# Hybrid RG-LRU, retention and gated feed-forward block: another order of ScalarE's work in the gelu branch, head 1's values by seven half-size products among the scores

## The chip, the core and the metric

The kernel runs on one core of one Trainium2 chip. The metric is device time in microseconds of one execution, from its launch to its end on the device. The kernel before was timed three times: 1058.52, 1058.54 and 1058.54 us, median 1058.54 us.

A core has a matrix engine (TensorE, PE in the profile, its weight loads PEld), a vector engine (VectorE, DVE), a scalar engine for activation functions (ScalarE, ACT), a general one (GpSimd, POOL), and queues from which DMAs are issued (here mostly SyncE's, SP). Data lies in SBUF; matmul results go to PSUM, eight banks of 512 float32 columns on 128 partitions.

## What is computed

One block of a hybrid language model on 512 tokens with 16 learned meta tokens in front (T = 528), model width 1024, in float32. Cut to what matters:

```python
xn = rms_norm(h, norm_mix_g)
u_rnn, u_gate, q, k, v, g_ret, ga, gb = jnp.split(xn @ w_in, IN_SPLITS, axis=-1)

xr = causal_dwconv(u_rnn, rnn_conv_w, rnn_conv_b)
hr = rg_lru(xr, rg_a_w, rg_a_b, rg_x_w, rg_x_b, lru_lambda)    # 10 blocks of 128 channels
o_a = hr * gelu(u_gate)

o = retention(rotary(q), rotary(k) * 256 ** -0.5, v)            # 4 heads, dk 256, dv 512
o_b = head_rms(o) * silu(g_ret)

mixed = sigmoid(ga) * (o_a @ w_branch_rnn) + sigmoid(gb) * (o_b @ w_branch_ret)
h = h + mixed @ w_out
gate, val = split(causal_dwconv(rms_norm(h, norm_ffn_g) @ w_up, ffn_conv_w, ffn_conv_b))
h = h + (gelu(gate) * val) @ w_down
out = rms_norm(h, norm_final_g)[:, 16:]
```

In rg_lru, r and i are sigmoids of two small products per block, log_a = -8 r softplus(-lambda), a = exp(log_a), and the state follows s_t = a s_(t-1) + sqrt(1 - a^2) i x_t.

## The kernel before

**Precision.** Each float32 operand is split into two float16 parts, high and low (`split`, lines 93 to 96: ScalarE copies the scaled value to float16, VectorE subtracts that from the scaled value). A product is the sum of three float16 products, high by high, high by low, low by high (`SPLIT`). Weights come by DMA into one of three raw buffers (`wraw`) and are split into tiles of a pool of ten (`wsp`).

**Weight units.** Every weight matrix is cut into units of about 1 MB in the order of use (`units`). A plain unit makes two tiles in two steps. A unit marked `fast` is used in a Strassen-like scheme: a product of 2 x 2 blocks by seven half-size products instead of eight, on sums of blocks. Its `fast_steps` (lines 243 to 281) are five: half a tile, a tile, the block sums on VectorE (lines 262 to 264, 2048 columns in all), and two more tiles of the sums, marked late. `tick` emits the next step if the tiles from the current unit to that one number at most `ahead`; `get` emits all steps that are still missing of a unit.

**Order by hand.** From the first products to line 754 a hand-written order holds (`manual_schedule`): TensorE, ScalarE and VectorE each issue these instructions in the order of the program text. Behind that a planner orders the instructions, and may also pull later ones forward, between those written by hand too.

**The recurrent branch, lines 685 to 706.** Ten blocks n: `conv_product` (48 matmuls) into one of four PSUM accumulators of two banks (`acc`, from n = 2 on), `conv_taps` (one ScalarE and three VectorE operations on those sums), `conv_split`, and with a lag of three blocks `rnn_gates` (two products of six matmuls each into two accumulators, two sigmoids on ScalarE, a multiplication). Then softplus(-lambda) is made from a series of small operations (lines 709 to 727), which gives `cneg` and `cpos`.

**The gelu branch, lines 730 to 743.** Ten rounds n: `project` (48 matmuls) into an accumulator, one `tick`, Gelu from PSUM into SBUF on ScalarE, in rounds 0 to 2 the gates of blocks 7 to 9, and by a table (`SPREAD`) for five blocks at once: `rnn_tanh` and `rnn_decay` (ScalarE Tanh, Exp, two VectorE operations), `rnn_root` (ScalarE Sqrt), and in round 7 `rnn_scan` for blocks 0 to 4 (VectorE: a product and a scan over 528 tokens). ScalarE loads a function table when the next function isn't in the one it holds.

**Rotary, lines 761 to 792.** Eight units (q and k of four heads), each two projections of 48 matmuls, six VectorE operations on them, two splits. `between(i)` puts a scan of blocks 5 to 9 behind units 0 to 4, and `branch_a` (the product with the gelu result, and its split).

**Scores and values, lines 804 to 955 and 1148 to 1159.** `scores(h)`: three groups of products of rotated k and q into accumulators; VectorE multiplies by the decay, then they are split. `values(h)` for heads 0 and 1: 96 matmuls of 512 columns and 16 for the last 16 tokens. `fast_values(h)` for heads 2 and 3 (lines 960 to 1017): seven products of 24 matmuls of 256 columns on sums of the tokens' blocks, which `make_forms(0)` and `make_forms(1)` (lines 847 to 866) make once for all: for each, four additions, four more sums, four splits. The order of the calls is:

```python
    scores(0)
    values(0)
    make_forms(0)
    scores(1)
    scores(2)
    make_forms(1)
    values(1)
    scores(3)
    psum_layout(acc=2, bank=4)
```

Then come `retention_out`, the gated heads, the mixing, the output projection and the feed-forward part, which the change leaves alone.

Of the kernel before, what the change touches and what calls it, by code (L numbers as in the profile page):

```python
# [1 line left out]

# [51 lines left out]
def hybrid_block_kernel(ctx, tc, x, meta, norm_mix_g, w_in, conv_w, conv_b, rg_a_w, rg_a_b,  # L54
# [625 lines left out]
    def rnn_scan(n):  # L680
        r, t, xr = part(half_r, n), part(half_t, n), part(half_x, n)
        nc.vector.tensor_mul(t, t, xr)
        nc.vector.tensor_tensor_scan(xr, r, t, 0.0, op0=ALU.mult, op1=ALU.add)
# [25 lines left out]
    lv = vt1[:, 70:80]  # L709
    sp = const.tile([P, 8, NR], F32, name="sp")  # L710
    nc.vector.tensor_scalar(sp[:, 0], lv, -1.0, 0.0, op0=ALU.mult, op1=ALU.max)
    nc.scalar.activation(sp[:, 1], lv, AF.Abs)
    nc.scalar.activation(sp[:, 2], sp[:, 1], AF.Exp, scale=-1.0)
    nc.vector.tensor_scalar_add(sp[:, 3], sp[:, 2], 2.0)
    nc.vector.reciprocal(sp[:, 4], sp[:, 3])
    nc.vector.tensor_mul(sp[:, 4], sp[:, 4], sp[:, 2])
    nc.vector.tensor_mul(sp[:, 5], sp[:, 4], sp[:, 4])
    nc.vector.memset(sp[:, 6], 1.0 / 15.0)
    for m in (13, 11, 9, 7, 5, 3, 1):
        nc.vector.tensor_mul(sp[:, 6], sp[:, 6], sp[:, 5])  # L720
        nc.vector.tensor_scalar_add(sp[:, 6], sp[:, 6], 1.0 / m)
    nc.vector.tensor_mul(sp[:, 6], sp[:, 6], sp[:, 4])
    nc.vector.scalar_tensor_tensor(sp[:, 7], sp[:, 6], 2.0, sp[:, 0], op0=ALU.mult, op1=ALU.add)
    cneg = const.tile([P, NR], F32, name="cneg")
    cpos = const.tile([P, NR], F32, name="cpos")
    nc.vector.tensor_scalar_mul(cneg, sp[:, 7], -8.0)
# [4 lines left out]
    SPREAD = ((rnn_tanh, 2, 0), (rnn_decay, 3, 0), (rnn_tanh, 4, 5), (rnn_decay, 5, 5), (rnn_root, 7, 0), (rnn_scan, 7, 0), (rnn_root, 9, 5))
    for n in range(NR):
        ps = acc("ps")
        u, col = u_ug[n // 2], (n % 2) * P
# [2 lines left out]
        nc.scalar.activation(part(gate_g, n)[:, :TQ], run_of(ps, HQ),
                             AF.Gelu_apprx_tanh, scale=1.0 / (SW * S_XN))
# [106 lines left out]
    x_form_t = {}

    def make_forms(g):

        if not x_form_t:
            for i in range(2):  # L850
                x_form_t[i] = xslot([P, 4, 4, TW], F16, f"xs{i}")
        ks = slice(2 * g, 2 * g + 2)
        t = {}
        for i in range(2):
            for j in range(2):
                v = t[i, j] = work.tile([P, 2 * TW], F32, name="xt", tag="w").rearrange("p (k c) -> p k c", k=2)
                k0, c0 = 4 * j + 2 * g, XF + TH * i
                nc.vector.tensor_tensor(v, xh[:, k0:k0 + 2, c0:c0 + TW], xl[:, k0:k0 + 2, c0:c0 + TW], op=ALU.add)
        a11, a12, a21, a22 = t[0, 0], t[0, 1], t[1, 0], t[1, 1]
        nc.vector.tensor_tensor(a22, a22, a21, op=ALU.subtract)  # L860
        nc.vector.tensor_tensor(a21, a11, a21, op=ALU.subtract)
        nc.vector.scalar_tensor_tensor(a11, a22, -1.0, a11, op0=ALU.mult, op1=ALU.subtract)
        nc.vector.scalar_tensor_tensor(a12, a11, -1.0, a12, op0=ALU.mult, op1=ALU.subtract)
        for i, v in enumerate((a12, a22, a11, a21)):
            xs = x_form_t[i // 2]
            split(xs[:, 2 * (i % 2), ks], xs[:, 2 * (i % 2) + 1, ks], v, 1.0)

# [91 lines left out]

    def fast_values(h):  # L960

# [4 lines left out]
        vt = vv[h] = {}  # L966
        pa, pe, pb, pt = bank("pa"), bank("pe"), bank("pb"), acc("pv")[:, 0]

        def product(ps, wf, xf_, first=False):
            for a in range(2):  # L970
                for tt in range(2):
                    for k in range(2):
                        for ax, aw in SPLIT:
                            nc.tensor.matmul(ps[:, TH * tt:TH * tt + TH], x_form(xf_, ax, 2 * a + k, tt * P, P),  # L974
                                             ws[a](wf, aw, k),
                                             start=first and (a, tt, k, ax, aw) == (0, 0, 0, 0, 0),
                                             stop=a == 1 and k == 1 and ax == 1, skip_group_check=True)
# [807 lines left out]
```

## Time and profile before

| | |
|---|---|
| median of three runs | 1058.54 us |
| the profiled execution, its own time | 1058.55 us |
| its span, first to last instruction | 1056.8 us |
| mean granted TensorE clock | 0.999 |
| TensorE busy, matmuls | 1038.8 us |
| VectorE busy | 872.0 us |
| ScalarE busy | 594.3 us |
| DMA moved | 111.52 MB, mean 106 GB/s |

The profile is one execution. Each row of a view in order of time gives the start in us from the span's beginning, the time in us, the engine, the line of the kernel, the operation, what it writes and reads, its shape, and how many instructions are merged into the row; in square brackets stands how long the engine was idle before, and whom the profile names as releaser. "issue" means that the profile shows nobody. A merged row's time is from the first start to the last end. Matmuls overlap in time, so that TensorE's pace is better read from the starts of its weight loads.

### The profile page before, as it was taken

How to read it: one execution, taken by the hardware profiler on the slowest of the kernel's cores; microseconds unless marked ns; L12 is line 12 of the kernel's file. 1: busy time of each engine (PE TensorE's matmuls, PEld its weight loads, DVE VectorE, ACT ScalarE, POOL GpSimd, SP SyncE). 2: the span in 40 equal slices, each digit the busy share in tenths (PEclk: the TensorE clock that was granted, in tenths of full speed). 3: DMA queues.
4: the chain of work that ended last, by engine and by line, in shares of the span. 5: the costliest groups of instructions: out<-in, count | busy, mean ns of one | idle time of the engine just before them, and what ended most of it. 6: DMA issues, size and time to landing. Idle time of an engine off the chain costs nothing.

```text
span 1056.8 us, 21446 instructions
## 1 busy us (share of the span) xinstructions
PE 1038.8 (98%) x9187; PEld 866.2 (82%) x9187; DVE 872.0 (83%) x1327; ACT 594.3 (56%) x942; POOL 6.9 (1%) x20
## 2 busy tenths in 40 slices
PE   8999999999999999999999999999999999999997
PEld 6888888875588888888888886588888888888884
DVE  6885799989669999997797785479989898988965
ACT  7558973444356758666454453375555555454432
POOL 2000000000000000000000000000000000000000
PEclk9999999999999999999999999999999999999999
DMA  9241253331013132334333355032433324114312
GB/s 295 94 132 58 81 180 120 123 120 41 1 41 113 49 106 74 102 111 154 102 115 120 111 209 180 1 120 81 160 102 99 120 81 144 58 61 145 96 41 80
DMA packets 109311, 111.52 MB, mean 106 GB/s; under 512 B 5674, under 2 KB 101136, under 8 KB 109216
## 3 DMA queue, kind: packets, MB, share of 16 engines
q1 hardware_dynamic: 108640, 109.74, 32.5%
q8 instruction: 72, 1.18, 0.5%
q10 hardware_dynamic: 288, 0.27, 0.1%
q0 software_dynamic: 288, 0.14, 0.1%
q14 instruction: 23, 0.19, 0.1%
HBM read 108.04 MB, written 2.10 MB: 104 GB/s over the span
## 4 chain that ended last, share of the span: by engine, by line
PE 74%; DVE 15%; ACT 8%; issue 2%; DMA 0%; ACTq 0%; DVEq 0%
PE ps L434 27%; PE P L1603 10%; PE pa L886 9%; DVE wt L95 4%; PE pe L886 4%; PE ps L1320 4%; PE pm L434 3%; PE ps L448 3%; PE pb L886 2%; PE ps L950 2%; PE pa L1490 2%; ACT wt L94 2%; PE ps L1040 2%; PE pa L974 1%; DVE raw L262 1%
## 5 line engine op out<-in xcount | busy, mean ns | idle before, releaser
L434 PEld LDWEIGHTS <-wt 128*128 128x128 f16 x3840 | 372.8, 97 | 53.4 <-issue 1.3
L95 DVE SCALAR_TENSOR_TENSOR wt<-raw,wt 128x1024 f16<-128x1024 f32 (+2 forms) x286 | 310.4, 1102 | 54.0 <-ACT wt L94 52.9
L94 ACT ACTIVATE wt<-raw 128x1024 f16<-128x1024 f32 (+2 forms) x286 | 267.8, 958 | 117.8 <-PE P L1603 23.1
L886 PEld LDWEIGHTS <-wt 128*128 128x128 f16 x2016 | 195.3, 97 | 32.4 <-issue 5.7
L434 PE MATMUL ps<-x2h,wt 128*128 128x258 f16 (+1 forms) x1184 | 196.2, 273 | 0.0
L434 PE MATMUL ps<-xh,wt 128*128 128x258 f16 (+4 forms) x1056 | 177.5, 275 | 1.6 <-DVE t L773 1.6
L434 PE MATMUL ps<-x2l,wt 128*128 128x256 f16 (+1 forms) x592 | 161.0, 272 | 0.0
L434 PE MATMUL ps<-xl,wt 128*128 128x256 f16 (+4 forms) x528 | 140.8, 274 | 0.0
L1603 PE MATMUL P<-wt,act 128*128 128x256 f16 x792 | 88.3, 273 | 0.0
L1603 PEld LDWEIGHTS <-act 128*128 128x128 f16 x792 | 77.4, 98 | 9.0
L886 PE MATMUL pa<-xs,wt 128*128 128x258 f16 x576 | 71.3, 273 | 1.9 <-ACT kept L892 1.5
L1468 DVE SCALAR_TENSOR_TENSOR cv<-ps,vt,cv 128x512 f32<-128x512 f32 x80 | 59.5, 747 | 9.1 <-ACT cv L1466 8.5
L434 PE MATMUL pm<-oa,wt 128*128 128x256 f16 (+1 forms) x480 | 54.1, 273 | 0.0
L262 DVE TENSOR_TENSOR raw<-raw 128x1024 f32<-128x1024 f32 x43 | 52.5, 1220 | 0.7
L886 PE MATMUL pa<-ob,wt 128*128 128x257 f16 x384 | 45.7, 274 | 0.6 <-ACT last L892 0.5
L1320 PE MATMUL ps<-wt,mx 128*128 128x512 f16 x192 | 44.3, 379 | 0.0
L950 PE MATMUL ps<-wt,xh 128*128 128x512 f16 x128 | 38.3, 379 | 0.7 <-ACT qk L94 0.5
L1466 ACT ACTIVATE cv<-ps,vt,vt 128x512 f32<-128x512 f32 x40 | 30.5, 766 | 11.9 <-PE ps L434 11.9
L1490 PEld LDWEIGHTS <-wt 128*128 128x128 f16 x336 | 32.6, 97 | 4.4
L1320 PEld LDWEIGHTS <-mx 128*128 128x128 f16 x192 | 17.6, 98 | 18.5
L94 ACT ACTIVATE qk<-t 128x514 f16<-128x514 f32 (+1 forms) x16 | 10.2, 638 | 39.6 <-DVE t L775 39.6
L448 PEld LDWEIGHTS <-wt 128*128 128x128 f16 x288 | 27.9, 97 | 5.0 <-issue 0.5
(327 smaller groups left out, 1504.5 us busy)
## 6 DMA issues: line engine op xcount, KB each, us to landing
raw<-in_w_in SPq DMA_DIRECT2D x36, 1024.0 KB, 5.1
raw<-in_w_up SPq DMA_DIRECT2D x24, 1024.0 KB, 5.2
raw<-in_w_down SPq DMA_DIRECT2D x48, 256.0 KB, 3.7
raw<-in_w_branch_ret SPq DMA_DIRECT2D x16, 512.0 KB, 4.9
raw<-in_w_in SPq DMA_DIRECT2D x12, 512.0 KB, 4.8
raw<-in_w_branch_rnn SPq DMA_DIRECT2D x8, 640.0 KB, 4.7
raw<-in_w_out SPq DMA_DIRECT2D x4, 1024.0 KB, 5.1
xin<-in_x SPq DMA_DIRECT2D x4, 512.0 KB, 5.8
```

Of the source, the lines that this page charges most:

```text
L94: a = nc.scalar.activation(hi, src, AF.Copy, scale=s)
L95: b = nc.vector.scalar_tensor_tensor(lo, src, s, hi, op0=ALU.mult, op1=ALU.subtract)
L262: nc.vector.tensor_tensor(pair, pair, rv[:, :, right].rearrange("p (h k) c -> p h k c", h=2), op=ALU.add)
L434: nc.tensor.matmul(half_of(ps, halves, hf), w(aw, k, col, P), src(ax, k, c0, n), start=k == 0 and (aw, ax) == (0, 0), stop=k == nk - 1 and ...
L448: mm = nc.tensor.matmul(half_of(ps, halves, hf), w(aw, k, col, P), src(ax, k, c0, n), start=k == 0 and (aw, ax) == (0, 0), stop=k == KD - ...
L886: nc.tensor.matmul(ps[:, :n], ws[k // 4](wf, aw, k % 4), src(xf_, ax, k), start=first and k == 0 and (aw, ax) == (0, 0), stop=k == last_k ...
L950: nc.tensor.matmul(pb, xf(ax, k, XF + j0, nb), w(aw, k % 4, 0, 512), start=i == 0, stop=i == 23)
L1320: nc.tensor.matmul(ps[:, n], mx[k][:, a, c0:c0 + P], wo[k // 2](aw, k % 2, n * 512, 512), start=k == 0 and (a, aw) == (0, 0), stop=k == ks ...
L1466: nc.scalar.activation(vv_, taps[2], AF.Identity, scale=vt2[:, 96 + ch:97 + ch], bias=bias)
L1468: nc.vector.scalar_tensor_tensor(vv_, taps[j], vt2[:, 48 * j + ch:48 * j + ch + 1], vv_, op0=ALU.mult, op1=ALU.add)
L1490: nc.tensor.matmul(ps[:, :258], w(wf, aw, k), x2_form(xf_, ax, k), start=first and k == 0 and (aw, ax) == (0, 0), stop=k == 3 and aw == 1, ...
L1603: nc.tensor.matmul(pd[:, 256 * tt:256 * tt + 256], t[:, ax, c0 + tt * P:c0 + tt * P + P], w(wf, aw, i), start=q % 6 == 0 and tt == 0 and i ...
```

## The change

- Softplus: its Abs and Exp are issued in round 2 of the recurrent branch, its VectorE operations, 18 instead of 24, three at a time behind `conv_taps` of rounds 3 to 7.
- Tanh of blocks 0 to 5 is issued in rounds 8 and 9 of the recurrent branch, of blocks 6 to 9 in rounds 0 to 2 of the gelu branch.
- Gelu: in rounds 5, 8 and 9 from PSUM as before; in the others ScalarE copies the sums to SBUF (`AF.Copy`), and Gelu is done later in place, in rounds 5 and 8. In a round the work of the tables `FIRST` and `THEN` stands ahead of that copy.
- The gates of blocks 8 and 9 both stand in round 1.
- Eight of ten scans are in the gelu branch (rounds 7 to 9), two are left in `between`.
- `make_forms(0)` stands in round 0 of the gelu branch, behind its `tick`; `make_forms(1)` behind `values(0)`.
- Head 1's weight units are `fast`, and `fast_values(1)` takes the place of `values(1)`: behind each product it lets one group of `scores(2)`, then of `scores(3)`, be issued. For it the PSUM layout with two accumulators and four single banks begins before it and not behind `scores(3)`; the products for the last tokens get a bank of their own. `ahead` is 12 there.

```diff
     def add_v(h):
-        if h >= 2:
-            u_v[h] = [unit(4, 512, [(2 * j, 0, kmaj(w_in, 4 * j + 2 * a, 2, o_v + 512 * h, 512)) for j in range(2)],
-                           fast=True) for a in range(2)]
+        if h == 0:
+            u_v[h] = [unit(4, 512, [(0, 0, kmaj(w_in, 4 * a, 4, o_v, 512))]) for a in range(2)]
             return
-        u_v[h] = [unit(4, 512, [(0, 0, kmaj(w_in, 4 * a, 4, o_v + 512 * h, 512))]) for a in range(2)]
+        u_v[h] = [unit(4, 512, [(2 * j, 0, kmaj(w_in, 4 * j + 2 * a, 2, o_v + 512 * h, 512)) for j in range(2)],
+                       fast=True) for a in range(2)]
...
+    def softplus_exp():
+        lv = vt1[:, 70:80]
+        nc.vector.tensor_scalar(sp[:, 0], lv, -1.0, 0.0, op0=ALU.mult, op1=ALU.max)
+        nc.scalar.activation(sp[:, 1], lv, AF.Abs)
+        nc.scalar.activation(sp[:, 2], sp[:, 1], AF.Exp, scale=-1.0)
+
+    def softplus_rest():
+        nc.vector.tensor_scalar_add(sp[:, 3], sp[:, 2], 2.0)
+        nc.vector.reciprocal(sp[:, 4], sp[:, 3])
+        nc.vector.tensor_mul(sp[:, 4], sp[:, 4], sp[:, 2])
+        yield
...
         conv_taps(n, ps)
+        if LAG <= n < 8:
+            next(series)
+        if n >= 8:
+            for i in range(3 * (n - 8), 3 * (n - 8) + 3):
+                rnn_tanh(i)
...
         if n == 2:
+            softplus_exp()
             tick()
...
+    def make_forms(g):
...
+        nc.vector.scalar_tensor_tensor(a12, a11, -1.0, a12, op0=ALU.mult, op1=ALU.subtract)
+        for i, v in enumerate((a12, a22, a11, a21)):
+            xs = x_form_t[i // 2]
+            split(xs[:, 2 * (i % 2), ks], xs[:, 2 * (i % 2) + 1, ks], v, 1.0)
...
-    SPREAD = ((rnn_tanh, 2, 0), (rnn_decay, 3, 0), (rnn_tanh, 4, 5), (rnn_decay, 5, 5), (rnn_root, 7, 0), (rnn_scan, 7, 0), (rnn_root, 9, 5))
+    FIRST = {0: (rnn_tanh, (6,)), 1: (rnn_tanh, (7,)), 2: (rnn_tanh, (8, 9)), 5: ("gelu", range(5)), 6: (rnn_root, range(5)), 7: (rnn_root, range(5, 10)),
+             8: ("gelu", (6, 7))}
+    THEN = {2: (rnn_decay, (0, 1)), 3: (rnn_decay, range(2, 6)), 4: (rnn_decay, range(6, 10)),
+            7: (rnn_scan, range(3)), 8: (rnn_scan, (3, 4)), 9: (rnn_scan, range(5, 8))}
+
+    def gate_gelu(i, src=None, s=1.0):
+        g = part(gate_g, i)[:, :TQ]
+        nc.scalar.activation(g, g if src is None else src, AF.Gelu_apprx_tanh, scale=s)
+
     for n in range(NR):
         ps = acc("ps")
         u, col = u_ug[n // 2], (n % 2) * P
         project(ps, get(u), col, xf, HQ, KD)
         tick()
-        nc.scalar.activation(part(gate_g, n)[:, :TQ], run_of(ps, HQ),
-                             AF.Gelu_apprx_tanh, scale=1.0 / (SW * S_XN))
-        if n < LAG:
-            rnn_gates(NR - LAG + n)
-        for f, n0, m0 in SPREAD:
-            if n == n0:
-                for i in range(m0, m0 + 5):
-                    f(i)
+        if n == 0:
+            make_forms(0)
+        for what in (FIRST, THEN):
+            f, ms = what.get(n, (None, ()))
+            for m in ms:
+                (gate_gelu if f == "gelu" else f)(m)
+        if n in (5, 8, 9):
+            gate_gelu(n, run_of(ps, HQ), 1.0 / (SW * S_XN))
+        else:
+            nc.scalar.activation(part(gate_g, n)[:, :TQ], run_of(ps, HQ), AF.Copy, scale=1.0 / (SW * S_XN))
+        for i in ((7,), (8, 9))[n] if n < 2 else ():
+            rnn_gates(i)
...
     def between(i):
-        if i < 5:
-            rnn_scan(5 + i)
+        if i < 2:
+            rnn_scan(8 + i)
...
-    scores(0)
+    rest(scores(0))
     values(0)
-    make_forms(0)
-    scores(1)
-    scores(2)
     make_forms(1)
-    values(1)
-    scores(3)
+    rest(scores(1))
     psum_layout(acc=2, bank=4)
+    ahead[0] = 12
+    fast_values(1, chain(scores(2), scores(3)))
     ahead[0] = 9
```

More of the change, by code (lines that the diff above doesn't have):

```diff
@@ L1 @@
 from contextlib import ExitStack, nullcontext
+from itertools import chain
 import concourse.bass as bass
@@ L683, in rnn_scan @@
         nc.vector.tensor_tensor_scan(xr, r, t, 0.0, op0=ALU.mult, op1=ALU.add)
+    cneg = const.tile([P, NR], F32, name="cneg")
+    cpos = const.tile([P, NR], F32, name="cpos")
+    sp = const.tile([P, 8, NR], F32, name="sp")
+    def softplus_exp():
[8 more added lines that the diff above has]
+        yield
+        nc.vector.tensor_mul(sp[:, 5], sp[:, 4], sp[:, 4])
+        nc.vector.tensor_scalar_mul(sp[:, 6], sp[:, 5], 1.0 / 15.0)
+        for m in (13, 11, 9, 7, 5, 3):
+            nc.vector.scalar_tensor_tensor(sp[:, 6], sp[:, 6], 1.0 / m, sp[:, 5], op0=ALU.add, op1=ALU.mult)
+            if m in (13, 7):
+                yield
+        nc.vector.scalar_tensor_tensor(sp[:, 6], sp[:, 6], 1.0, sp[:, 4], op0=ALU.add, op1=ALU.mult)
+        yield
+        nc.vector.scalar_tensor_tensor(sp[:, 7], sp[:, 6], 2.0, sp[:, 0], op0=ALU.mult, op1=ALU.add)
+        nc.vector.tensor_scalar_mul(cneg, sp[:, 7], -8.0)
+        nc.vector.tensor_scalar_mul(cpos, sp[:, 7], 8.0)
+        yield
+    series = softplus_rest()
     LAG = 3
@@ L706, in hybrid_block_kernel @@
             conv_split(n)
[L709 to L726, printed above, removed]
@@ L727, in hybrid_block_kernel @@
-    nc.vector.tensor_scalar_mul(cpos, sp[:, 7], 8.0)
-    ahead[0] = 6
-    SPREAD = ((rnn_tanh, 2, 0), (rnn_decay, 3, 0), (rnn_tanh, 4, 5), (rnn_decay, 5, 5), (rnn_root, 7, 0), (rnn_scan, 7, 0), (rnn_root, 9, 5))
+    x_form_t = {}
+    def make_forms(g):
+        if not x_form_t:
+            for i in range(2):
+                x_form_t[i] = xslot([P, 4, 4, TW], F16, f"xs{i}")
+        ks = slice(2 * g, 2 * g + 2)
+        t = {}
+        for i in range(2):
+            for j in range(2):
+                v = t[i, j] = work.tile([P, 2 * TW], F32, name="xt", tag="w").rearrange("p (k c) -> p k c", k=2)
+                k0, c0 = 4 * j + 2 * g, XF + TH * i
+                nc.vector.tensor_tensor(v, xh[:, k0:k0 + 2, c0:c0 + TW], xl[:, k0:k0 + 2, c0:c0 + TW], op=ALU.add)
+        a11, a12, a21, a22 = t[0, 0], t[0, 1], t[1, 0], t[1, 1]
+        nc.vector.tensor_tensor(a22, a22, a21, op=ALU.subtract)
+        nc.vector.tensor_tensor(a21, a11, a21, op=ALU.subtract)
+        nc.vector.scalar_tensor_tensor(a11, a22, -1.0, a11, op0=ALU.mult, op1=ALU.subtract)
+        nc.vector.scalar_tensor_tensor(a12, a11, -1.0, a12, op0=ALU.mult, op1=ALU.subtract)
+        for i, v in enumerate((a12, a22, a11, a21)):
+            xs = x_form_t[i // 2]
+            split(xs[:, 2 * (i % 2), ks], xs[:, 2 * (i % 2) + 1, ks], v, 1.0)
@@ L802, in hybrid_block_kernel, with rest @@
     SCP = [(0, SOFF[0]), (1, SOFF[1]), (2, SOFF[2]), (2, SOFF[2]), (2, SOFF[2])]
+    def rest(run):
+        for _ in run:
+            pass
     def scores(h):
@@ L832, in group @@
                 split(sb[:, 0, o:o + n], sb[:, 1, o:o + n], f[:, :n], 1.0)
-        group([(0, 0, 0, 257), (1, 0, 257, 257)])
-        group([(0, 1, 0, T - I0[1]), (1, 2, 0, T - I0[2])])
-        group([(0, 3, 0, T - I0[3]), (1, 4, 0, T - I0[4])])
+        yield group([(0, 0, 0, 257), (1, 0, 257, 257)])
+        yield group([(0, 1, 0, T - I0[1]), (1, 2, 0, T - I0[2])])
+        yield group([(0, 3, 0, T - I0[3]), (1, 4, 0, T - I0[4])])
     xlast = const.tile([P, KD, 2, NM], F16, name="xlast")
@@ L843, in hybrid_block_kernel @@
     vv, oraw, rstd, ob, ob_a11 = {}, {}, {}, [], []
[L845 to L866, printed above, removed]
     def x_form(nm, a, k, c0, n):
@@ L958, in hybrid_block_kernel, with fast_values @@
     nc.vector.tensor_scalar_mul(xneg, xlast[:, 0:4], -1.0)
-    def fast_values(h):
+    def fast_values(h, others=()):
         ws = [get(u) for u in u_v[h]]
@@ L966, in fast_values @@
         vt = vv[h] = {}
-        pa, pe, pb, pt = bank("pa"), bank("pe"), bank("pb"), acc("pv")[:, 0]
+        others = iter(others)
+        pa, pe, pb = bank("pa"), bank("pe"), bank("pb")
+        pt = bank("pv") if h == 1 else acc("pv")[:, 0]
         def product(ps, wf, xf_, first=False):
@@ L978, in product @@
             tick()
+            next(others, None)
         def keep(ps):
@@ L1034, in retention_out @@
                     o = SOFF[b] + s0 - I0[b] - SCP[b][1]
-                    if h < 2 or b == 4:
+                    if h == 0 or b == 4:
                         vd = vt[b][:, va, d * P:(d + 1) * P]
@@ L1212, in mix_first @@
         mix_a.append(m)
-    def rest(run):
-        for _ in run:
-            pass
     def gate_a(i, run=None):
```

## The prediction

> **What bounds the kernel now.** I read the page's busy shares and its chain first, then the weight loads in order of time, then ScalarE and VectorE beside them.
>
> ```profile
> span 1056.8 us, 21446 instructions
> ...
> PE 1038.8 (98%) x9187; PEld 866.2 (82%) x9187; DVE 872.0 (83%) x1327; ACT 594.3 (56%) x942; POOL 6.9 (1%) x20
> ...
> PE 74%; DVE 15%; ACT 8%; issue 2%; DMA 0%; ACTq 0%; DVEq 0%
> ```
>
> TensorE sets the end. A change pays only by taking matmul time away or by closing a gap between matmuls; ScalarE, at 56%, pays only where TensorE waits for it. Every f16 matmul here has its own weight load, so the loads (PEld) in order of time show each gap:
>
> ```profile
> 80.86 5.28 PEld L434 LDWEIGHTS <-wt 128*128 128x128 f16 x48
> 86.15 1.33 PEld L434 LDWEIGHTS <-gw 128*128 128x128 f16 x12
> 87.50 5.28 PEld L434 LDWEIGHTS <-wt 128*128 128x128 f16 x48
> 92.79 1.33 PEld L434 LDWEIGHTS <-gw 128*128 128x128 f16 x12
> ...
> 100.77 68.99 PEld L434 LDWEIGHTS <-wt 128*128 128x128 f16 x624
> 170.64 10.74 PEld L434 LDWEIGHTS <-wt 128*128 128x128 f16 x96 [0.88 <-DVE t L773]
> 182.64 42.74 PEld L434 LDWEIGHTS <-wt 128*128 128x128 f16 x384 [1.26 <-issue]
> ```
>
> The gelu branch (ten rounds, the first at 80.86) has no gap, though ScalarE is full there: TensorE runs on over 624 loads from 100.77. So **relieving ScalarE is worth nothing by itself**. The gaps, 0.88 and 1.26 us, come in the rotary stage, the first put down to VectorE.
>
> **The change part by part.** *The sums in the gelu branch.* Up to the end of that branch each engine keeps the program's order. Rows of ScalarE, then of VectorE:
>
> ```profile
> 85.61 0.20 ACT L712 ACTIVATE sp<-vt 128x10 f32<-128x10 f32 x1
> ...
> 87.23 1.04 ACT L94 ACTIVATE wt<-raw 128x1024 f16<-128x1024 f32 x1
> ...
> 89.58 0.60 ACT L737 ACTIVATE rnn<-ps 128x514 f32<-128x514 f32 x1
> 90.20 1.28 ACT L663 ACT_TABLE_LOAD   x1
> 91.50 0.70 ACT L663 ACTIVATE rnn<-ps,vt 128x528 f32<-128x528 f32 x1
> 92.09 0.69 ACT L663 ACTIVATE gi<-ps,vt 128x528 f32<-128x528 f32 x1
> ...
> 103.60 3.23 ACT L668 ACTIVATE rnn<-rnn,cpos 128x528 f32<-128x528 f32 x5
> ...
> 128.46 0.60 ACT L737 ACTIVATE rnn<-ps 128x514 f32<-128x514 f32 x1
> ...
> 244.28 1.75 ACT L94 ACTIVATE xs<-xt 128x544 f16<-128x544 f32 x3
> ```
>
> ```profile
> 91.69 1.22 DVE L95 SCALAR_TENSOR_TENSOR wt<-raw,wt 128x1024 f16<-128x1024 f32 x1
> 92.82 0.70 DVE L665 TENSOR_TENSOR rnn<-rnn,gi 128x528 f32<-128x528 f32 x1
> ...
> 113.14 0.70 DVE L674 TENSOR_TENSOR a<-rnn 128x528 f32<-128x528 f32 x1
> 113.87 0.71 DVE L675 SCALAR_TENSOR_TENSOR rnn<-a,rnn 128x528 f32<-128x528 f32 x1
> ...
> 236.27 0.72 DVE L858 TENSOR_TENSOR xt<-xh,xl 128x544 f32<-128x544 f16 x1
> ...
> 238.16 1.99 DVE L858 TENSOR_TENSOR xt<-xh,xl 128x544 f32<-128x544 f16 x3
> ...
> 243.53 0.72 DVE L863 SCALAR_TENSOR_TENSOR xt<-xt 128x544 f32<-128x544 f32 x1
> ```
>
> The order shows at 91.69: the low half of a weight split whose high half ended at 88.27 waits until the small softplus operations are through. In the new round 0 ScalarE gets the weight split, then the four splits of make_forms(0), tanh(6), and only then the copy that empties round 0's sums from PSUM. The first of the four splits needs a12, the last of eight VectorE operations. Worked out:
>
> - The weight split takes the place of L712 at 85.61 and ends at 86.65. Its low half starts at 86.69 and holds VectorE 1.13 (91.69 to 92.82), to 87.82.
> - Eight operations follow at 0.635 each (three end to end in 1.99, the last taking 0.72), one of them 0.10 later because it reads the result just made (113.14 to 113.87 against 0.63). a12 is there at 87.82 + 7 x 0.635 + 0.10 + 0.72 = 93.1. Until then ScalarE stands still.
> - Four splits at 0.55 each (1.75 for three) run to 95.3, tanh(6) at 0.63 (3.23 for five) to 96.0, the copy at 0.60 to 96.6.
>
> TensorE meets this at 92.79. PSUM has four accumulators, and then all are held: round 0's sums, the two gates of block 7, round 1's sums. The gates of block 8 come next and wait for the copy, from 92.79 to 96.6: **3.8 us**. Behind the copy ScalarE has the sigmoids of block 7 (96.45, 97.04), round 1's weight split (97.63), tanh(7) and round 1's copy, which ends at 99.8. The fourth of the gate products of blocks 8 and 9 (0.67 each, half of 1.33) waits for that one: it could start at 96.6 + 3 x 0.67 = 98.6, so 1.25 more. Round 2 starts at 100.5 instead of 92.79 + 4 x 0.67 = 95.5: **+5.0 us**. Bounds of this unseen wait: 0 if the copy does not queue behind the splits; 7.7 if the eight operations take what they took at 236.27 to 244.25 among others (8.0 instead of 5.3). I take 5.0, since the hand-written order puts nothing between them. Later rounds carry no gates; a copy there may lie three rounds behind.
>
> *Tanh, softplus, in-place gelu, table loads.* Most table loads (1.28 each) go and seven 0.60 operations come; ScalarE bounds nothing in that branch apart from the wait above: 0. The 18 small series operations run three to a block in a hole like this one, at 0.21 a step:
>
> ```profile
> 79.78 0.71 DVE L95 SCALAR_TENSOR_TENSOR xs<-rnn,xs 128x528 f16<-128x528 f32 x1 [0.71 <-ACT xs L94]
> 88.44 0.17 DVE L721 TENSOR_SCALAR sp<-sp 128x10 f32<-128x10 f32 x1
> 88.65 0.17 DVE L720 TENSOR_TENSOR sp<-sp 128x10 f32<-128x10 f32 x1
> 39.18 0.64 ACT L94 ACTIVATE xs<-rnn 128x528 f16<-128x528 f32 x1 [2.76 <-DVE rnn L647]
> ```
>
> 3 x 0.21 = 0.63 fits under 0.71; without that cover it would be some 3 us of VectorE, not of TensorE. Abs, exponential and table load, 1.7, fit into the 2.76 before 39.18.
>
> *Scans moved ahead.* Three of the five scans between rotary units go into the gelu branch:
>
> ```profile
> 137.80:182.64 44.84, 43.26 (x387) 37.17 (x385) 44.84 (x57) 20.31 (x26) 0.00 (x0) 1.00 0.45 149
> 182.64:225.40 42.76, 42.73 (x384) 37.19 (x385) 39.81 (x57) 18.45 (x26) 0.00 (x0) 1.00 0.43 139
> 133.55 1.26 DVE L683 TENSOR_TENSOR_SCAN rnn<-rnn 128x528 f32<-128x528 f32 x1
> ```
>
> In these window rows (length, then TensorE, loads, VectorE) VectorE is full up to 182.64, and free for 3 us after. A scan and its product cost about 1.9, three 5.7, well over the 2.14 of both gaps. Nothing else is late there: the next unit's accumulators come free with that same VectorE work. **-2.1 us.** Bounds 0 and -2.1, for the stage has no other gap to close.
>
> *Head 1's values.* Chain pieces of the plain form, then of the seven products of head 2, then windows of the stage and of heads 2 and 3:
>
> ```profile
> 260.05 15.38 PE ps L950 x71
> 275.43 0.98 PE ps L942 x16
> 335.60 0.86 PE pv L1008 x25
> 339.19 2.62 PE pe L974 x24
> 225.40:285.20 59.80, 58.87 (x369) 30.92 (x367) 50.16 (x101) 23.77 (x46) 0.00 (x0) 1.00 0.08 27
> 320.00:341.70 21.70, 20.65 (x212) 17.44 (x210) 19.78 (x25) 13.38 (x20) 0.00 (x0) 1.00 0.34 104
> 368.40:389.90 21.50, 20.56 (x211) 17.36 (x210) 19.73 (x26) 13.63 (x19) 0.00 (x0) 1.00 0.32 105
> ```
>
> Plain: 96 matmuls at 0.217 plus 0.98 for the last 16 tokens = 21.8. New: 7 x 2.62 = 18.3, plus 40 small ones (25 in 0.86) at 1.4 = 19.7. **-2.1 us**, if nothing waits. VectorE, at 1.13 per 1024 columns, gets per unit 1.5 more low halves and 2048 columns of sums (4.0; two units 8.0) and three additions of 512 (1.7), and loses twelve operations of make_forms (7.6): some 2.1 into 9.6 free (59.80 less 50.16). Scores stand between the products and give VectorE time. Bounds: -2.1, and 0, for heads 2 and 3 take 21.7 and 21.5 for this very work, no less than the plain form. I take -2.1, because there VectorE is free for only 2 us.
>
> **Sum:** the profiled execution took 1058.55 (span plus 1.75; the median is 1058.54). 1058.55 + 5.0 - 2.1 - 2.1 = **1059.4**. A measurement of this kernel can tell about 0.2%, 2.1 us, from no change, so I forecast no difference.
>
> **The rivals.**
>
> *The half-size products wait for their weights* as heads 2 and 3 do: then the third term is 0 and the time 1061.5, slower. It decides itself at the third product, whose form is cut last and whose buffers come free only when head 0's values are done; in between lie scores(1) (8076 columns at 0.217 per 512: 3.4), two products (5.2) and two score groups (7116 columns: 3.0), 11.6 us. For it: the two windows. Against it: 9.6 us free.
>
> *ScalarE's queue does not hold the copy back*, so the sums cost nothing: 1058.55 - 2.1 - 2.1 = 1054.4, faster. For it: round 6 ends on TensorE at 100.77 + 192 x 0.1106 = 122.0 (68.99 for 624 loads), its result leaves PSUM at 128.46, and no gap follows. Against: in rounds 0 and 1 gates take the accumulators that gave round 6 its time.
>
> *The wait slows the clock.* Quoted windows show a granted clock of 1.00, gaps up to 1.26 included; 3.8 us of idling is not in the trace. Were the 24 gate matmuls behind it (2.67) at half pace, the time would be 1062.1. The Trainium skill, "TensorE: Matmul & The Clock Gate", section "HAM oscillation — how this bites in real kernels", says that an idle gap over about 3.4 us halves the clock; no row of before bears on it.
>
> *VectorE stays late in the rotary stage*: the second term is 0, 1061.5. Against: 5.7 us less to do, and TensorE arrives 5.0 later.
>
> **How the numbers follow.** Forecast 0.50 (of it 0.03 faster, 0.39 same, 0.08 slower), products waiting 0.17 (0.06 same, 0.11 slower), no hold-back 0.22 (faster), clock 0.06 (slower), rotary 0.05 (0.02 same, 0.03 slower). Together faster 0.25, same 0.47, slower 0.28. The forecast's own range is 1057.0 to 1061.5: planner-placed work after the branch can shift a gap of 0.5 to 1.2 either way. The range given, 1054.0 to 1062.0, takes in most of the other cases, the middle of the no-hold-back case too.
>
> **What would show it.** Right: a gap of about 3.8 us before the gates of block 8 and 1.2 before the last gate of block 9, both released by ScalarE's copies; round 2 some 5 us late; no gap over 0.3 near 170 and 182 (shifted by 5); head 1's 168 products in 18.3 us of their own. Wrong: no gap before round 2, or gaps over 1 us among head 1's products.

## The result and the profile after

The changed kernel takes **1061.28 us** (median of 14 runs, 1060.23 to 1061.87) against 1058.58 us for the kernel before on the same chip: ratio 1.0023, 95% interval 1.0016 to 1.003. That is 2.7 us slower, just over what a measurement can tell from no change. The forecast was 1059.4 us.

The page of the changed kernel: its span, the busy shares, the granted clock over 40 slices, and the shares of the chain that ended last.

```profile
span 1059.5 us, 21649 instructions
...
PE 1039.5 (98%) x9283; PEld 875.2 (83%) x9283; DVE 881.8 (83%) x1332; ACT 591.1 (56%) x947; POOL 6.9 (1%) x20
...
PEclk9998999999999999999999999999999999999999
...
PE 83%; DVE 11%; ACT 4%; issue 2%; ACTq 0%; DVEq 0%
```

ScalarE lost 3 us of work and VectorE gained 10, yet the span grew by 2.7: the shares don't tell why. One digit does: the fourth slice of PEclk, around 80 to 106 us, fell to 8. So the weight loads are read in order of time again (start, duration, engine, line, operation, operands, count, idle time before it):

```profile
85.93 1.33 PEld L435 LDWEIGHTS <-gw 128*128 128x128 f16 x12
87.27 5.28 PEld L435 LDWEIGHTS <-wt 128*128 128x128 f16 x48
92.56 0.10 PEld L435 LDWEIGHTS <-gw 128*128 128x128 f16 x1
96.75 4.94 PEld L435 LDWEIGHTS <-gw 128*128 128x128 f16 x23 [4.09 <-issue]
101.77 128.01 PEld L435 LDWEIGHTS <-wt 128*128 128x128 f16 x1152
229.79 3.50 PEld L875 LDWEIGHTS <-qk 128*128 128x128 f16 x30
...
287.41 7.58 PEld L1075 LDWEIGHTS <-v 128*128 128x128 f16 x96
```

Row 101.77 runs on over 1152 loads to the scores at 229.79: both gaps of the rotary stage are gone. Of the kernel before, beside the rows shown with the prediction, the first load of the scores and the first after scores and values:

```profile
225.39 3.50 PEld L820 LDWEIGHTS <-qk 128*128 128x128 f16 x30
...
285.23 7.57 PEld L1040 LDWEIGHTS <-v 128*128 128x128 f16 x96
```

The two lists, taken stage by stage, give the whole difference of 2.7 us between the spans:

| stretch, by the starts of its loads | before | after | difference |
|---|---|---|---|
| up to the end of round 1's projection | 92.79 | 92.56 | -0.23 |
| gates of blocks 8 and 9, up to round 2 (before: 4 x 0.67 for the same products) | 2.68 | 9.21 | +6.53 |
| round 2 to the scores (before: 225.39 less 95.47) | 129.92 | 128.02 | -1.90 |
| scores and values of heads 0 and 1 | 59.84 | 57.62 | -2.22 |
| the rest of the span | 771.6 | 772.1 | +0.5 |

The +0.5 us of the last row falls behind TensorE's last matmuls, which start at 1048.80 us before and at 1051.04 after, 2.24 us apart. The loss has one place, the gelu branch, and two parts there. The first is the idle time of 4.09 us before the gates' second load. The second stands in the row behind it: 23 loads in 4.94 us, where the same loads went at 12 in 1.33 us in block 7. The windows of the changed kernel (length, then busy time of TensorE, loads, VectorE, ScalarE, GpSimd, then granted clock, DMA share, GB/s) show why:

```profile
90.00:92.50 2.50, 2.50 (x25) 2.19 (x24) 2.40 (x4) 0.00 (x0) 0.00 (x0) 1.00 0.00 0
92.50:96.70 4.20, 0.33 (x4) 0.15 (x2) 3.36 (x6) 3.40 (x7) 0.00 (x0) 0.80 0.00 0
95.00:96.00 1.00, 0.00 (x0) 0.00 (x0) 1.00 (x3) 1.00 (x3) 0.00 (x0) 0.52 0.00 0
...
100.00:101.00 1.00, 1.00 (x6) 0.72 (x5) 0.08 (x1) 1.00 (x3) 0.00 (x0) 0.50 0.00 0
...
102.00:103.00 1.00, 1.00 (x11) 0.88 (x10) 0.13 (x1) 0.87 (x2) 0.00 (x0) 1.00 1.09 387
```

The granted clock was 1.00 up to the gap and fell to 0.50 within it, at about 95.0; behind the gap it stayed there for some 5 us. In a stretch of 1 us TensorE gets through 6 products at 0.50 and 11 at 1.00. What filled the gap is on ScalarE, then on VectorE, in the changed kernel; the last row is TensorE's, the matmuls behind the gap:

```profile
93.30 2.30 ACT L95 ACTIVATE xs<-xt 128x544 f16<-128x544 f32 x4 [6.87 <-DVE xt L764]
95.50 0.72 ACT L669 ACTIVATE rnn<-rnn,cpos 128x528 f32<-128x528 f32 x1
96.12 0.58 ACT L793 ACTIVATE rnn<-ps 128x514 f32<-128x514 f32 x1
...
99.34 0.60 ACT L793 ACTIVATE rnn<-ps 128x514 f32<-128x514 f32 x1
```

```profile
87.60 2.63 DVE L759 TENSOR_TENSOR xt<-xh,xl 128x544 f32<-128x544 f16 x4
...
92.54 0.72 DVE L764 SCALAR_TENSOR_TENSOR xt<-xt 128x544 f32<-128x544 f32 x1
```

```profile
96.75 5.34 PE L435 MATMUL ps<-xs,gw 128*128 128x264 f16 x24 [3.92 <-ACT rnn L793]
```

ScalarE, the engine that the change relieves, stands still for 6.87 us in round 0: its next instruction is the first split of the tokens' sums, and that waits for the eighth VectorE operation, which ends at 93.26. Behind the four splits and tanh(6) stands the copy (L793) that empties round 0's accumulator; it ends at 96.70, and TensorE resumes at 96.75. The last row above, of the matmuls behind the gap, names that copy as their releaser; the row of the loads shows nobody ("issue").

### The profile page after: what moved, and what is told of

Same layout as the page of the kernel before. It is cut to its first block, busy times and chain, and to the rows that moved or that the text cites. A ratio compares the mean times of both kernels' runs of the same rounds, so it can differ in the third digit from the quotient of the medians.

```text
span 1059.5 us, 21649 instructions
## 1 busy us (share of the span) xinstructions
PE 1039.5 (98%) x9283; PEld 875.2 (83%) x9283; DVE 881.8 (83%) x1332; ACT 591.1 (56%) x947; POOL 6.9 (1%) x20
## 4 chain that ended last, share of the span: by engine, by line
PE 83%; DVE 11%; ACT 4%; issue 2%; ACTq 0%; DVEq 0%
PE ps L435 35%; PE P L1632 10%; PE pa L918 9%; PE pe L918 4%; PE ps L1349 4%; PE pm L435 3%; DVE wt L96 3%; PE ps L449 3%; PE pb L918 2%; PE pa L1008 2%; PE pa L1519 2%; PE ps L1075 2%; ACT wt L95 1%; PE pe L1008 1%; DVE raw L263 1%
## 5 line engine op out<-in xcount | busy, mean ns | idle before, releaser
L96 DVE SCALAR_TENSOR_TENSOR wt<-raw,wt 128x1024 f16<-128x1024 f32 (+2 forms) x290 | 314.7, 1101 | 57.5 <-ACT wt L95 56.2
L95 ACT ACTIVATE wt<-raw 128x1024 f16<-128x1024 f32 (+2 forms) x290 | 271.4, 958 | 127.9 <-DVE raw L263 22.9
L263 DVE TENSOR_TENSOR raw<-raw 128x1024 f32<-128x1024 f32 x45 | 54.9, 1221 | 0.7
L1008 PEld LDWEIGHTS <-xs 128*128 128x128 f16 x288 | 27.8, 98 | 5.9 <-issue 2.8
L1075 PE MATMUL ps<-sc,v 128*128 128x257 f16 (+4 forms) x384 | 31.6, 236 | 0.0
```

What stands on the lines that cost most here:

```text
L95: a = nc.scalar.activation(hi, src, AF.Copy, scale=s)
L96: b = nc.vector.scalar_tensor_tensor(lo, src, s, hi, op0=ALU.mult, op1=ALU.subtract)
L263: nc.vector.tensor_tensor(pair, pair, rv[:, :, right].rearrange("p (h k) c -> p h k c", h=2), op=ALU.add)
L1075: nc.tensor.matmul(ps[:, hf, s0 - lo_i:257], vd, st[SCP[b][0]][:, sa, o:o + hi_i - s0], start=i == 0, stop=i == len(todo) - 1)
```

## The experiments

All ratios are against the kernel before on the same chip, which took 1058.51 to 1058.61 us in every comparison.

| kernel | median us | ratio, 95% interval |
|---|---|---|
| changed | 1061.28 | 1.0023, 1.0016 to 1.003 |
| copy_first | 1060.68 | 1.0018, 1.0009 to 1.0027 |
| fill_gap | 1060.04 | 1.0015, 1.0006 to 1.0024 |
| split_order | 1058.87 | 1.0001, 0.9992 to 1.0011 |
| forms_round3 | 1058.55 | 0.9999, 0.999 to 1.0009 |
| series_gelu | 1058.00 | 0.9995, 0.9985 to 1.0004 |
| gelu_only | 1057.97 | 0.9994, 0.9985 to 1.0003 |
| series_only | 1057.74 | 0.9992, 0.9983 to 1.0002 |
| relief_only | 1056.76 | 0.9983, 0.9974 to 0.9992 |
| scans_late | 1056.70 | 0.9982, 0.9973 to 0.9992 |
| back_plain | 1056.61 | 0.9982, 0.9973 to 0.9992 |
| forms_back | 1054.76 | 0.9964, 0.995 to 0.9978 |
| back_scans | 1054.66 | 0.9964, 0.9951 to 0.9977 |

### What holds TensorE in the gelu branch

**split_order** cuts the sum that is ready first, and a12 last.

```diff
-        for i, v in enumerate((a12, a22, a11, a21)):
+        for i, v in ((1, a22), (3, a21), (2, a11), (0, a12)):
```

> make_forms splits its four sums in the order in which they are made (a22, a21, a11, a12) instead of a12 first. ScalarE then has its splits done about 1.6 us sooner and round 0's copy ends near 95.1 instead of 96.7: a gap of about 2.6 us instead of 4.1. If the wait alone counts: 1061.3 - 1.6 = 1059.7, with the 24 gate products behind the gap still taking 5.0 us. If a gap of 4.1 us halves the clock and one of 2.6 does not: the 24 products run at full pace, only the last of them waits some 1.3 us for round 1's copy, about 3.9 us lost in all instead of 6.5, so 1058.7 with a granted clock of 0.999.

**copy_first** puts round 0's copy ahead of the sums.

```diff
         if n == 0:
+            nc.scalar.activation(part(gate_g, n)[:, :TQ], run_of(ps, HQ), AF.Copy, scale=1.0 / (SW * S_XN))
             make_forms(0)
...
-        else:
+        elif n > 0:
             nc.scalar.activation(part(gate_g, n)[:, :TQ], run_of(ps, HQ), AF.Copy, scale=1.0 / (SW * S_XN))
```

> Round 0's copy out of PSUM stands ahead of make_forms(0), all else as in the changed kernel. If only that copy holds TensorE up, the gap goes and the time is 1054.8. If any of the four accumulators does, the first gate product of block 8 starts at once and the second waits for the sigmoid of block 7, which is still behind the splits: a gap of about 3.6 us one product later, and a time near 1060 (1059.9 at full clock, 1060.5 with the clock halved for a while).

The weight loads of split_order, with the two gaps:

```profile
95.32 2.01 PEld L435 LDWEIGHTS <-gw 128*128 128x128 f16 x18 [2.46 <-issue]
98.56 0.55 PEld L435 LDWEIGHTS <-gw 128*128 128x128 f16 x5 [1.23 <-issue]
```

A window of it just behind the first gap:

```profile
95.30:96.30 1.00, 0.98 (x9) 0.86 (x9) 0.70 (x2) 1.00 (x2) 0.00 (x0) 1.00 0.00 0
```

The weight loads of copy_first, and its matmuls behind the gap:

```profile
92.86 0.77 PEld L435 LDWEIGHTS <-gw 128*128 128x128 f16 x7
97.16 3.62 PEld L435 LDWEIGHTS <-gw 128*128 128x128 f16 x17 [3.52 <-issue]
...
97.16 4.12 PE L435 MATMUL ps<-xs,gw 128*128 128x264 f16 x18 [3.35 <-ACT rnn L664]
```

A window of it 1 us behind the gap:

```profile
98.00:99.00 1.00, 1.00 (x6) 0.72 (x5) 0.76 (x2) 1.00 (x2) 0.00 (x0) 0.50 0.00 0
```

In split_order the gap shrinks from 4.09 to 2.46 us because ScalarE starts to cut before a12 is there, the clock stays at 1.00 behind it in the profiled execution, and the predicted second wait, for round 1's copy, comes into sight with 1.23 us. The median falls by 2.4 us. (The profile, at 1058.48 us, is one of four runs at 1058.33 to 1058.48; the other six took 1058.80 to 1059.29 at a mean clock lower by 0.001.) So the order of ScalarE's queue makes the gap. In copy_first the copy is out of the way, and TensorE gets just one gate product (6 loads) further before it stands still for 3.52 us: the accumulators of block 7's gates are still held then, since their sigmoids (L664, the releaser named) stand behind the same splits. The prediction let two copies alone set the waits; in truth each reader of the four accumulators that stands behind the splits is a holder.

### What the slow clock costs

**fill_gap** leaves the wait where it is, but gives TensorE 34 more matmuls in it, into columns of round 1's accumulator that nobody reads, so that nothing is left out of the computation.

```diff
-        project(ps, get(u), col, xf, HQ, KD)
+        wv = get(u)
+        project(ps, wv, col, xf, HQ, KD)
+        for i in range(34 if n == 1 else 0):
+            nc.tensor.matmul(ps[:, 0, 0:250], wv(0, i % KD, col, P), xf(0, i % KD, XF, 250), start=True, stop=True,
+                             skip_group_check=True)
```

> The changed kernel with 34 more matmuls of 250 columns behind round 1's own, into columns of its accumulator that nobody reads: about 3.7 us of work on TensorE that lies in the gap of 4.1 us and delays nothing. If the idling halves the clock for the gate products behind it, the clock stays at 0.999, the 24 products wait only for round 1's copy (about 1.3 us), and every run is as fast as the faster group of the changed kernel, 1060.3. If the products behind the gap are slow for another reason, nothing changes: 1061.3, in two groups of runs.

Its weight loads, the added ones (L785) first:

```profile
92.67 3.63 PEld L785 LDWEIGHTS <-wt 128*128 128x128 f16 x34
96.32 0.10 PEld L435 LDWEIGHTS <-gw 128*128 128x128 f16 x1
96.86 2.01 PEld L435 LDWEIGHTS <-gw 128*128 128x128 f16 x18 [0.44 <-issue]
100.10 0.55 PEld L435 LDWEIGHTS <-gw 128*128 128x128 f16 x5 [1.23 <-issue]
```

The window behind the filled gap:

```profile
97.00:101.00 4.00, 2.95 (x27) 2.42 (x26) 1.93 (x2) 4.00 (x7) 0.00 (x0) 1.00 0.00 0
```

The other 23 loads of the gates start at 96.86, 0.1 us later than in the changed kernel, but go at full pace; then the 1.23 us wait shows. The median is 1.24 us better than the changed kernel's. In the profiles the count agrees: from the first matmul behind the gap to round 2's first load the changed kernel took 5.02 us at half pace (96.75 to 101.77), fill_gap 3.80 at full pace with the second wait (96.86 to 100.66), 1.22 less. The waits themselves cost the rest, 6.53 - 1.22 = 5.3 us. The 1.24 us is a difference of medians: the changed kernel's times fall into two groups (last section), and the lower one is only 0.2 to 0.7 us above fill_gap's median.

### Where else the sums could stand

**forms_back** takes `make_forms(0)` back to the values; **forms_round3** issues it three rounds later, where no gates compete for accumulators.

```diff
         tick()
-        if n == 0:
-            make_forms(0)
...
     values(0)
+    make_forms(0)
     make_forms(1)
```

> make_forms(0) goes back behind the values of head 0, ahead of make_forms(1); all else as in the changed kernel. The gelu branch has no gap. If VectorE has room for the 7.6 us among scores and values: 1054.8, the same as with the sums in round 3. If it has not, head 1's products wait by up to 2 us, about 1056.8, and the half of the sums in the gelu branch is worth that.

```diff
-        if n == 0:
+        if n == 3:
             make_forms(0)
```

> make_forms(0) moves from round 0 to round 3 of the gelu branch, where no gates follow; all else is as in the changed kernel (1061.3 us). Theory, ScalarE's queue stands at the first split of the sums while gates hold the accumulators: the gap of 4.1 us before the gates of block 8 and the half clock behind it go, together 6.5 us, so 1054.8 and a granted clock of 0.999. Rival, both gates of round 1 or the copies behind other work are to blame whatever the sums do: the gap stays, about 1061. A second question is decided with it: if the rotary gaps of 0.88 and 1.26 us closed only because TensorE came 6.5 us late, they open again and the time is about 1056.9.

Weight loads of forms_back:

```profile
92.65 2.68 PEld L435 LDWEIGHTS <-gw 128*128 128x128 f16 x24
95.34 127.96 PEld L435 LDWEIGHTS <-wt 128*128 128x128 f16 x1152
223.32 3.50 PEld L873 LDWEIGHTS <-qk 128*128 128x128 f16 x30
...
280.89 7.58 PEld L1073 LDWEIGHTS <-v 128*128 128x128 f16 x96
```

One row of 1152 loads from 95.34 to 223.32 without a gap, and scores and values in 57.57 us, as short as in the changed kernel with the sums among them. At 1054.76 us this kernel is faster than both. The sums in the gelu branch therefore cost 1061.28 - 1054.76 = **6.5 us**, the size of the row in the table above, and at the values they cost nothing that can be measured.

Weight loads of forms_round3 at its only large gap:

```profile
161.45 65.81 PEld L435 LDWEIGHTS <-wt 128*128 128x128 f16 x576 [2.34 <-DVE t L824]
```

Its windows around that gap:

```profile
159.50:161.40 1.90, 0.00 (x0) 0.00 (x0) 1.90 (x4) 0.00 (x0) 0.00 (x0) 1.00 0.81 278
161.40:163.00 1.60, 1.55 (x8) 1.11 (x9) 1.60 (x3) 0.63 (x1) 0.00 (x0) 0.54 0.04 10
```

The gap in the gelu branch is gone, and another comes some 65 us later: VectorE, which has the sums in its way and so comes late to the rotary stage, is busy throughout the window (1.90 of 1.90) while TensorE does nothing, and then the clock is at half again. The kernel loses 3.8 us against forms_back and stands where the kernel before does. So the gelu branch is the wrong place by two reasons, not one: early in it the sums block accumulators, later in it they take VectorE's time that the rotary stage needs. In the changed kernel the second cost doesn't show. That this is because TensorE itself comes 6.5 us late to the rotary stage is an inference; no run tries it.

### What the other parts are worth

**back_scans** is forms_back with three scans put back behind rotary units; **back_plain** is forms_back with head 1's values in the plain form and the old order of calls; **relief_only** is back_plain with the scans put back as well, so that of the change only ScalarE's new order is left, with softplus made early and the gates of blocks 8 and 9 in one round. The early softplus relieves VectorE too: the 24 small operations that stood ahead of the gelu branch are gone, and 16 (not 18, as written above) stand in the recurrent branch.

```diff
-            7: (rnn_scan, range(3)), 8: (rnn_scan, (3, 4)), 9: (rnn_scan, range(5, 8))}
+            7: (rnn_scan, range(3)), 8: (rnn_scan, (3, 4))}
...
-        if i < 2:
-            rnn_scan(8 + i)
+        if i < 5:
+            rnn_scan(5 + i)
```

> The kernel with make_forms(0) back among the values (1054.8), and the scans of blocks 5 to 7 back between the rotary units as before. If these three scans make VectorE late there: the gaps of 0.88 and 1.26 us come back, 1056.9. If the softplus series, the tanh or the gelu order closed them: 1054.8.

```diff
-        if h == 0:
+        if h < 2:
...
     make_forms(0)
-    make_forms(1)
     rest(scores(1))
+    rest(scores(2))
+    make_forms(1)
+    values(1)
+    rest(scores(3))
     psum_layout(acc=2, bank=4)
-    ahead[0] = 12
-    fast_values(1, chain(scores(2), scores(3)))
```

> The kernel with make_forms(0) back among the values (1054.8), and head 1's values by the plain product again, in the old order of the calls. If the seven half-size products are worth the matmul time they save (2.1 to 2.2 us) and nothing else: 1057.0, and 1.6 to 2.1 us below the kernel before. If they are worth less, as in heads 2 and 3 with their waits: about 1055.

> Of the change only what relieves ScalarE and the softplus series: tanh earlier, gelu in place, fewer table loads, gates of blocks 8 and 9 in one round; the sums, head 1's values and the three scans are as before. If ScalarE bounds nothing in the gelu branch: 1058.6, no difference from before. If it did, up to 2 us faster.

The steps between these medians are the parts of the change. Moved scans: forms_back against back_scans +0.1, relief_only against back_plain -0.15, so **nothing** either way. Half-size products: 1056.61 - 1054.76 = **1.85 us**. ScalarE's new order with the early softplus: 1058.51 - 1056.76 = **1.75 us**. This relief was priced at nothing in the prediction, and the scans at the whole of this gain. The loads of back_plain show where the 1.85 us come from: 59.83 us for scores and values instead of the 57.57 of forms_back.

```profile
223.21 3.50 PEld L873 LDWEIGHTS <-qk 128*128 128x128 f16 x30
...
283.04 7.56 PEld L1073 LDWEIGHTS <-v 128*128 128x128 f16 x96
```

That is 2.26 us. Of it 2.12 are still there at TensorE's last matmuls, which start at 1044.50 us in forms_back and at 1046.62 in back_plain; the rest goes behind them. From the start of the last matmuls to the end of the span it is 8.4 to 8.5 us in the profiles of all seven kernels with the half-size products of head 1, and 8.0 to 8.1 in the seven without. Why is open.

### How relief on ScalarE reaches TensorE

ScalarE keeps TensorE waiting nowhere in the gelu branch of the kernel before, and yet the new order (with the early softplus) closes both gaps of the rotary stage, at 170 and 182 us. The loads of relief_only run through there in one row, to the scores at 223.69:

```profile
95.72 127.95 PEld L435 LDWEIGHTS <-wt 128*128 128x128 f16 x1152
```

Between the two stands VectorE. Its busy time is the third number behind the length in these windows, first of the kernel before, then of relief_only:

```profile
100.00:120.00 20.00, 20.00 (x184) 17.62 (x182) 10.24 (x14) 19.87 (x27) 0.00 (x0) 1.00 0.16 54
...
140.00:160.00 20.00, 20.00 (x182) 17.37 (x180) 20.00 (x24) 11.36 (x15) 0.00 (x0) 1.00 0.56 176
```

```profile
100.00:120.00 20.00, 20.00 (x184) 17.63 (x183) 17.85 (x24) 17.63 (x26) 0.00 (x0) 1.00 0.20 61
...
140.00:160.00 20.00, 20.00 (x182) 17.38 (x180) 20.00 (x25) 4.64 (x5) 0.00 (x0) 1.00 0.74 238
```

VectorE's first scan in relief_only:

```profile
126.82 1.25 DVE L684 TENSOR_TENSOR_SCAN rnn<-rnn 128x528 f32<-128x528 f32 x1
```

From 140 to 180 us VectorE has no free time in either. Before that, from 100 to 120, it is half idle in the kernel before, with ScalarE full (19.87 of 20): the decays and roots that VectorE needs come late. In relief_only it does 7.6 us more there; its first scan starts at 126.82 and not at 133.55, and by 140 us seven scans have started instead of three. What VectorE hasn't done by 140 us it does in the rotary stage, ahead of the operations that TensorE waits for. In the kernel before, five branch products in a row stand there, and the operations that read the accumulators for the next unit come only behind them, from 181.24 on; TensorE's load behind the second gap starts at 182.64:

```profile
178.23 3.09 DVE L750 TENSOR_TENSOR rnn<-rnn 128x514 f32<-128x514 f32 x5
181.24 0.69 DVE L774 TENSOR_TENSOR t<-ps,rope 128x514 f32<-128x514 f32 x1
```

Three runs on the kernel before asked which edit does it. **gelu_only** copies the sums of rounds 0 to 4 and does their Gelu in place in round 6; **series_only** makes softplus early, in rounds 2 to 7 of the recurrent branch; **series_gelu** does both.

```diff
+        if n == 6:
+            for i in range(5):
+                g = part(gate_g, i)[:, :TQ]
+                nc.scalar.activation(g, g, AF.Gelu_apprx_tanh)
         nc.scalar.activation(part(gate_g, n)[:, :TQ], run_of(ps, HQ),
-                             AF.Gelu_apprx_tanh, scale=1.0 / (SW * S_XN))
+                             AF.Copy if n < 5 else AF.Gelu_apprx_tanh, scale=1.0 / (SW * S_XN))
```

> The kernel before with one edit: rounds 0 to 4 of the gelu branch copy their sums out of PSUM, and Gelu is done for them in place in round 6, so that ScalarE spends fewer table loads on going back and forth between Gelu and Sigmoid or Exp. Softplus, tanh, scans, sums and values are as before. New theory, ScalarE's lateness is handed to VectorE (decays and scans start late) and from there to TensorE in the rotary stage: the gaps of 0.88 and 1.26 us close, about 1056.6. Rival, the softplus series on VectorE made it late: 1058.5, no difference.

```diff
         conv_taps(n, ps)
+        if LAG <= n < 8:
+            next(series)
...
         if n == 2:
+            softplus_exp()
             tick()
...
-    nc.scalar.activation(sp[:, 1], lv, AF.Abs)
-    nc.scalar.activation(sp[:, 2], sp[:, 1], AF.Exp, scale=-1.0)
```

> The kernel before with the softplus operations alone moved into rounds 2 to 7 of the recurrent branch, three at a time behind the taps; all else as before. New theory, ScalarE's lateness is what counts: most of the gaps stay, 1058 to 1058.5 (ScalarE is spared one table load of 1.28 us by it). Rival, the 5 us of small operations on VectorE made it late: 1056.6.

> Both single edits together on the kernel before: softplus earlier and Gelu in place for rounds 0 to 4. Each alone closed the first rotary gap (0.88) and left the second (1.26). If what counts is how much ScalarE's and VectorE's queues are relieved, the second goes as well: 1056.7. If the second depends on where decays and scans stand in the rounds, which neither edit moves: 1057.5 to 1058.

All three are 0.6 to 0.8 us below the kernel before, none surely different from it. Their loads behind the place of the second gap, in the order gelu_only (with the row ahead of it, which runs over the place of the first gap), series_only, series_gelu:

```profile
100.74 79.83 PEld L434 LDWEIGHTS <-wt 128*128 128x128 f16 x720
182.09 42.74 PEld L434 LDWEIGHTS <-wt 128*128 128x128 f16 x384 [1.52 <-issue]
```

```profile
181.60 42.74 PEld L434 LDWEIGHTS <-wt 128*128 128x128 f16 x384 [1.26 <-issue]
```

```profile
182.08 42.74 PEld L434 LDWEIGHTS <-wt 128*128 128x128 f16 x384 [1.53 <-issue]
```

In each the first gap is gone and the second stays; where Gelu was moved it has grown, from 1.26 to 1.52 and 1.53 us. VectorE's time from 100 to 120 us fits that: 11.00 us in series_gelu, hardly more than the 10.24 before, and by 140 us three scans have started, as before.

```profile
100.00:120.00 20.00, 20.00 (x184) 17.59 (x183) 11.00 (x14) 19.36 (x27) 0.00 (x0) 1.00 0.20 59
```

What closes the second gap is thus in the part that relief_only has beyond series_gelu: tanh in the recurrent branch, decays in rounds 2 to 4, roots in rounds 6 and 7, both gates in round 1, other rounds for part of Gelu and of the scans. Which of these it is was not tried. **scans_late** was to test the other half of the account by holding the scans back until round 9 in relief_only:

```diff
-            7: (rnn_scan, range(3)), 8: (rnn_scan, (3, 4))}
+            9: (rnn_scan, range(5))}
```

> The relieved kernel (1056.8) with its first five scans in round 9 instead of rounds 7 and 8; nothing else moves. If the rotary gaps are closed because the scans are done sooner: they come back, 1058.5 or more. If they are closed because ScalarE has less to do: 1056.8.

It is the same as relief_only (1056.70 against 1056.76), but tells nothing: VectorE had so little ahead of the scans that they ran at the same time from their later place too.

```profile
126.72 2.40 DVE L684 TENSOR_TENSOR_SCAN rnn<-rnn 128x528 f32<-128x528 f32 x2
```

That ScalarE's new order with the early softplus is worth 1.75 us is shown. How much of it is ScalarE's relief alone is not: series_only, which mainly moves small operations of VectorE out of the way of the gelu branch, comes to 0.8 us by itself, gelu_only to 0.6, and both together to 0.6. That the way goes by VectorE's earlier work is read from the traces, and no run takes that step alone. forms_round3 fits it: there VectorE has the sums to do as well, its first scan starts at 133.30, and the gap in the rotary stage is put down to it.

## Why the prediction was right or wrong

- **The sums' hold-back: right, and mis-sized.** Predicted: the first copy's end at 96.6, a wait of 3.8 us, then 1.25 us for round 1's copy, together 5.0. Measured: 96.70, 4.09 between the loads, and 1.23 wherever the clock stayed up (split_order, fill_gap). Both waits are released by ScalarE's copies, as predicted. The term came to 6.5 us by forms_back: by fill_gap's median 1.2 of that is the clock and about 5.3 are the waits, longer than predicted mainly because TensorE arrives 0.23 us earlier.
- **The rival of the clock came true on top of the forecast.** It got a chance of 0.06 and was priced at 2.67 us for 24 products. From the first of them to round 2 it took 5.02 us instead of 2.68, 2.3 more, but half pace hides the second wait, which leaves 1.2 net by fill_gap.
- **"Relieving ScalarE is worth nothing by itself": wrong.** The step looked for a wait of TensorE on ScalarE inside the gelu branch and found none. It didn't follow lateness from there through VectorE into the next stage. Measured, together with the early softplus: 1.75 us.
- **"Scans moved ahead, -2.1 us": the gaps close, but by another cause.** Both gaps are gone in the changed kernel (-1.90 from round 2 to the scores). Without the move (back_scans, relief_only) they are gone as well, so the move is worth nothing, and this term and the one before have exchanged their values. That the sum hardly notices is luck: one mechanism was left out, and another was credited with its gain.
- **Head 1's products, -2.1 us: right.** The stage became 2.22 us shorter, the median 1.85. The rival, that the products wait for their weights as in heads 2 and 3, fell: the changed kernel's largest gap among them is 0.69 us, before the first.
- **The other rivals.** No hold-back fell: the gap stands in the trace. VectorE late in the rotary stage did not happen in the changed kernel, and did happen in forms_round3, where TensorE is on time.
- **The sum.** Predicted +5.0 - 2.1 - 2.1 = +0.9 us; by the runs +6.5 - 1.75 - 1.85 = +2.9, measured +2.7. The time, 1061.28 us, is 1.9 above the forecast and just inside the forecast's own range (to 1061.5). The 2.1 us that the prediction called no difference were passed by 0.6; without the slow clock's 1.2 they would have held.

## What to carry to other kernels

Before work is put into another engine's free time, look at what stands behind it in that engine's queue: a split that waits for eight VectorE operations holds each later instruction that empties an accumulator, and what was gained in ScalarE's time came back as waiting on its queue. An engine that nobody visibly waits for may still be late for someone: where a downstream engine is half idle in one stage and full in the next, earlier input can be worth the waits that its lateness causes further on (here 1.75 us of 7.6 us of idle time). And a change in several parts is taken apart before it is judged: here one part, at 6.5 us, hid the 3.8 us that the others bring.

## What the runs showed of the hardware

- **A gap of 2 us can drop the clock.** The granted clock fell to 0.50 at gaps between loads of 4.09 us (changed), 3.52 (copy_first) and 2.34 us (forms_round3), and stayed at 1.00 behind 2.46 us in the profile of split_order. In windows of 0.1 us the fall comes 2.2, 2.1 and 2.1 us after the end of TensorE's last matmul before the gap, and the clock is back 6.8, 6.8 and 3.4 us after the fall; split_order's idle time between matmuls was 2.28 us. The Trainium skill, "TensorE: Matmul & The Clock Gate", section "HAM oscillation — how this bites in real kernels", gives idle gaps over about 3.4 us as the condition; here the clock had fallen in all three before that time was up, and a drop at 2.34 us beside none at 2.46 shows that the gap's length alone does not decide.
- **The same kernel's times fall into two groups.** The times of the changed kernel lie at 1060.23 to 1060.73 us with a mean clock of 0.997 or 0.998, or at 1061.26 to 1061.87 with 0.996, and those of copy_first and split_order split in the same way; fill_gap, without the long gap, has all its times within 1059.89 to 1060.41. The profile shown is one of the upper group (1061.26); the lower group was not profiled, so that its clock behind the gap is not seen.
